# The step size's projection of a hybrid decoder step: from split products on normalized features to plain float32 on the residual stream, in four column groups

## The chip, the cores and the metric

The kernel runs on one core of one Trainium2 chip. The metric is the device time of one execution in microseconds. Before the change it is 954.13 us, the median of three runs (953.25 to 955.27). Beside the times there is one profiled execution, read by views: a page, and questions to its trace (timelines by engine, waits, stretches of time). In these views PE is TensorE's matmul, PEld its weight load, DVE is VectorE, ACT ScalarE, POOL GpSimd, SP SyncE with its DMA queue.

## The reference

One layer of a decoder: a half-step feed-forward stage, a mixer of two parallel parts (a causal pooling mixer and a state-space mixer), and a second half-step feed-forward stage, with 512 prompt tokens and 8 single new tokens, 1024 features, all in float32. The change touches one small product: the last 16 columns of the mixer's input projection, which become the step size of each of the 16 heads.

```python
def _rms_norm(x, g):
    xf = x.astype(jnp.float32)
    y = xf * lax.rsqrt(jnp.mean(xf * xf, axis=-1, keepdims=True) + EPS)
    return (y * g.astype(jnp.float32)).astype(x.dtype)
...
    h = h + 0.5 * _swiglu(_rms_norm(h, ffn1_norm[l]), ...)
    m, p, c, s = _hybrid_mixer(_rms_norm(h, mix_norm[l]), ...)
...
    proj = h @ w_in
    u_pool, z, xbc, dt_raw = jnp.split(
        proj, [POOL_DIM, POOL_DIM + SSD_DIM, POOL_DIM + SSD_DIM + CONV_DIM], axis=-1)
...
    dt = jax.nn.softplus(dt_raw.astype(jnp.float32) + dt_bias.astype(jnp.float32))
```

So the raw step size is `dt_raw = (h * g * r) @ w_dt`, with `g` the norm's 1024 factors and `r` one number for each token.

## The kernel before

Features lie on the 128 partitions, in eight tiles (`k` or `d` from 0 to 7); tokens lie along the free axis, 520 of them in two halves of 260 (`HALVES`). The residual stream is the tile `h`, whose first columns hold the vectors of factors (`vec`).

Most products are made of split operands. A weight unit of 128x1024 is loaded into a staging tile `raw` (four slots in rotation), cast by ScalarE into a high part (`whi`, or `thi` in every third unit) and subtracted by VectorE into a low part (`wlo`, `tlo`; L141). The tiles of the parts come from rotating homes (`weight_homes`). Each product is then three matmuls: high x high, high x low, low x high (`mm3`, L151, L154, L155). The normalized features are split in the same way: `prep` (L179) scales `h` by the norm's factor on ScalarE into `xh` (L182), takes the rest on VectorE into `xl` (L183), squares `h` on ScalarE (L193) and adds the squares on VectorE into `acc` (L194). The factor `r` of each token is applied after the products.

The stage around the change is the seam between the first feed-forward stage and the mixer. The down products `dn` of the first stage run over the eight output tiles; after each one VectorE scales the sum (`td`, L618), adds it to `h` (L623) and `prep` follows. Then the mixer begins: it opens a pool `mx` (`mp`) in the room that the first stage gives back, loads its constants on SyncE's queue (L909 to L922), and computes the step size's raw value:

- `wdt`, 128 x 8 x 16, is loaded into a slot of `raw` (L946). `w48`, in a rotating weight home, holds for each feature tile 48 columns: the high part of the 16 weights, 16 zeros, the low part. It is zeroed by GpSimd (L949), filled by ScalarE (L950) and VectorE (L951).
- For each half and each `k` there are two matmuls: all 48 columns with `xh` (L957), and the first 16 with `xl` (L956, L959). In PSUM, partitions 0 to 15 then hold the high weights' sums and 32 to 47 the low ones'.
- `rstds` makes `r`: a product of `ones` with `acc` (L210, plain float32), a square root on ScalarE (L213), a reciprocal on VectorE (L214).
- `dv`, 48 x 520, is the PSUM sum times `r` (L963). `token_dt` (L970) multiplies it with the selecting matrix `sel`, 48 x 16: two unit matrices over each other, with zeros between. This product adds the two parts and turns tokens onto partitions.

After the projection come the input products `inbc`, `inx` and so on (`inproj`, L929), each of 48 matmuls, by the plans `CONV_PLAN` and `GATE_PLAN`. The order of instructions on each engine is set by a scheduler that works from a model of times when the program is built; on the chip every engine runs its own instructions in that order, and waits for others by semaphores. A tile of a pool whose room was another's waits for the last use of that one.

Of the kernel before, what the change touches and what calls it, by code (L numbers as in the profile page):

```python
# [10 lines left out]
F32 = mybir.dt.float32  # L11
F32R = mybir.dt.float32r
AF = mybir.ActivationFunctionType
ALU = mybir.AluOpType
# [3 lines left out]
P = 128  # L18
# [3 lines left out]
NT = SEQ + NS  # L22
HB = NT // 2
HALVES = (slice(0, HB), slice(HB, NT))
KD = D // P
# [3 lines left out]
NH = 16  # L29
# [29 lines left out]
VEC = {}  # L59
# [9 lines left out]
def tile_trunk_step(ctx: ExitStack, tc: tile.TileContext, ins: dict, outs: dict):  # L69
# [733 lines left out]

    ps[0] = tc.alloc_tile_pool(name="ppm", bufs=8, space=PSUM, reuse_waits="tile")
    mixer(tc, ins, outs, dict(locals()))
    f2["xg"].release()
    xa[0].release()
# [90 lines left out]
def mixer(tc, ins, outs, e):  # L898
    nc = tc.nc
    cst, act, wp, tmp, dr, pool = (e[x] for x in ("cst", "act", "wp", "tmp", "dr", "pool"))  # L900
    ones, queued, squared = e["ones"], e["queued"], tuple(e["added"])
    bank, load_unit, mm3, mm_low_last, ws, v, rstd, rstds, vec, h, nx2, raw_tile, open_f2, fin, fill = (
        e[x] for x in ("bank", "load_unit", "mm3", "mm_low_last", "ws", "v", "rstd", "rstds", "vec", "h", "nx2", "raw_tile",
                       "open_f2", "fin", "fill"))
    xh, xl, _, r = nx2[0]
    xa = e["xa"][0]
    mp = pool("mx", "right")
# [2 lines left out]
    nc.sync.dma_start(out=ident, in_=ins["ident"])  # L910
    tri = mp.tile([P, P], F32, tag="tri", name="tri")
    nc.sync.dma_start(out=tri, in_=ins["tri"])
    sel = mp.tile([48, NH], F32, tag="sel", name="sel")
    nc.sync.dma_start(out=sel, in_=ins["sel"])
    rcnt = mp.tile([P, PAST], F32, tag="rcnt", name="rcnt")
    nc.sync.dma_start(out=rcnt, in_=ins["rcnt"])
    hv = mp.tile([P, 2, NH], F32, tag="hv", name="hv")
# [27 lines left out]

    wdt = raw_tile("dt")[:, : KD * NH].rearrange("p (k h) -> p k h", k=KD)  # L946
    nc.sync.dma_start(out=wdt, in_=ins["w_dt"])
    w48 = e["weight_homes"](1024, "w48", wp, 3, ("whi", "wlo"))[0][:, : KD * 48].rearrange("p (k h) -> p k h", k=KD)
    nc.gpsimd.memset(w48.bitcast(F32), 0.0)  # L949
    nc.scalar.copy(w48[:, :, :NH], wdt)  # L950
    nc.vector.tensor_tensor(out=w48[:, :, 32:48], in0=wdt, in1=w48[:, :, :NH].bitcast(F32), op=ALU.subtract)  # L951
    dtb = [bank(f"dt{b}") for b in range(2)]
    for b, hs in enumerate(HALVES):
        for k in range(KD):
            if k:
                nc.tensor.matmul(dtb[b][:NH, :HB], w48[:, k, :NH], xl[:, k, hs], start=False, stop=False)  # L956
            nc.tensor.matmul(dtb[b][:48, :HB], w48[:, k], xh[:, k, hs], start=k == 0, stop=k == KD - 1)  # L957
            if not k:
                nc.tensor.matmul(dtb[b][:NH, :HB], w48[:, k, :NH], xl[:, k, hs], start=False, stop=False)  # L959
    rstds(nx2[0], "mx")  # L960
    dv = mp.tile([48, NT], F32, tag="h0", bufs=4, name="dv")
    for b, hs in enumerate(HALVES):
        nc.vector.tensor_tensor(out=dv[:, hs], in0=dtb[b][:48, :HB], in1=r[:48, hs], op=ALU.mult)  # L963
    tok = mp.tile([P, 2, NC + 1, NH], F32, tag="tok", name="tok")
    scr_dt = dr.tile([NH, NS], F32, name="scr_dt")
    scr_acs = dr.tile([NC * NH, CH], F32, name="scr_acs")
# [519 lines left out]
```

## Time and profile before

| | |
|---|---|
| median of three runs | 954.13 us |
| lowest, highest | 953.25, 955.27 us |
| span of the profiled execution, first to last instruction | 951.9 us |
| instructions | 19681 |
| mean granted TensorE clock | 0.997 |
| DMA, mean over the span | 145 GB/s |
| the projection's matmuls (L956, L957, L959), starts | 351.96 to 356.06 us |
| the sums of squares (L210), starts | 355.50 to 356.40 us |
| `dv` (L963), starts | 361.17 and 361.79 us |
| selecting product (L974), starts | 368.18 to 369.2 us |

A line of a timeline reads: start in us from the span's start, duration in us, engine, line, operation, tile written <- tiles read, shape, count, and in brackets the idle time ahead of it with what ended it. Rows that follow each other with the same name are merged, with their count. A matmul in plain float32 shows as two records of one instruction. Since matmuls are pipelined and the ends of their records are modelled, the distance between starts is their price, and not the length of a record.

### The profile page before, as it was taken

What the parts mean: (1) busy time and instruction counts of PE and PEld (TensorE: products, weight loads), DVE (VectorE), ACT (ScalarE), POOL (GpSimd) and SP (SyncE); (2) the same over time, 40 slices, a digit from 0 to 9 for tenths busy, and PEclk for the clock granted to TensorE, in tenths of its full rate; (3) what the DMA queues carried; (4) which work ended last, traced back from release to release, by engine and by line L of the source; (5) the groups of instructions that cost most, each with busy time, mean ns of one, the idle gap of its engine ahead of it and who ended that gap; (6) DMA issues with size and microseconds to landing.
All of it is one profiled execution on the core that took longest, in us unless ns stands there. A gap on an engine that the chain in (4) does not pass through costs nothing.

```text
span 951.9 us, 19681 instructions
## 1 busy us (share of the span) xinstructions
PE 942.5 (99%) x7674; PEld 925.9 (97%) x7674; DVE 852.7 (90%) x1462; ACT 635.7 (67%) x1179; POOL 148.3 (16%) x230
## 2 busy tenths in 40 slices
PE   9999999999999999999999999999999999999996
PEld 8999999999999999999999999999999999999996
DVE  6899899998988688789998998999999999999886
ACT  7777756677566455485668735777776676766774
POOL 0011100100100000046251100111112101122120
PEclk9999999999999999999999999999999999999998
DMA  7666554455553343354264453556666655776552
GB/s 205 187 166 150 143 151 135 115 140 156 134 155 95 86 134 122 92 180 138 91 184 133 141 114 115 138 122 160 163 173 176 163 146 144 171 194 185 145 180 91
DMA packets 53995, 138.35 MB, mean 145 GB/s; under 512 B 7750, under 2 KB 15878, under 8 KB 53902
## 3 DMA queue, kind: packets, MB, share of 16 engines
q1 hardware_dynamic: 39918, 104.19, 34.2%
q0 software_dynamic: 13712, 32.78, 18.7%
q8 instruction: 60, 0.98, 0.4%
q14 instruction: 33, 0.27, 0.1%
q10 hardware_dynamic: 272, 0.13, 0.0%
HBM read 129.74 MB, written 7.34 MB: 144 GB/s over the span
## 4 chain that ended last, share of the span: by engine, by line
PE 44%; DVE 2%; issue 1%; POOL 1%; DMA 1%; ACT 1%; DVEq 0%; ACTq 0%; POOLq 0%
PE A L160 8%; PE BE L160 6%; PE wo L160 5%; PE A L165 4%; PE BE L165 3%; PE wo L165 2%; PE P L311 1%; PE dh L155 1%; PE dh L151 1%; PE dh L154 1%; POOL zs L1068 1%; PE inz L151 1%; PE inz L154 1%; PE inz L155 1%; DMA room<-in_state_ssm 1%
## 5 line engine op out<-in xcount | busy, mean ns | idle before, releaser
L504 ACT COPY ac<-A 128x260 f32<-128x260 f32 x85 | 31.6, 372 | 35.4 <-PE A L155 17.3
L433 DVE TENSOR_TENSOR s<-raw 128x1024 f32<-128x1024 f32 x39 | 47.6, 1222 | 4.4 <-DMA raw<-in_w2gu 2.8
L504 ACT COPY ac<-BE 128x260 f32<-128x260 f32 x41 | 15.4, 376 | 33.6 <-PE BE L165 17.7
L151 PE MATMUL inx<-xh_mx,whi_inx 128*128 128x260 f32 x112 | 31.8, 284 | 0.0
L154 PE MATMUL inx<-xl_mx,whi_inx 128*128 128x260 f32 x112 | 31.6, 282 | 0.0
L155 PE MATMUL inx<-xh_mx,wlo_inx 128*128 128x260 f32 x112 | 31.6, 282 | 0.0
L1027 DVE SCALAR_TENSOR_TENSOR A<-U,h,A 128x544 f32<-128x544 f32 x36 | 29.0, 807 | 1.6 <-ACT A L1025 1.2
L311 PE MATMUL P<-x,raw 128*128 128x260 f32 x128 | 28.9, 385 | 0.2 <-DMA raw<-in_w1gu 0.2
L311 PEld LDWEIGHTS P<-x,raw 128*128 128x128 f32 x128 | 24.4, 192 | 4.2 <-DMA raw<-in_w1gu 0.6
L160 PE MATMUL wo<-catg,whi_wo 128*128 128x260 f32 x192 | 27.4, 285 | 0.0
L1193 ACT ACTIVATE so<-br,sxdt 128x128 f32<-128x128 f32 x64 | 22.8, 376 | 5.8 <-DVE room L1195 5.2
L160 PEld LDWEIGHTS wo<-catg,whi_wo 128*128 128x128 f32 x192 | 24.8, 188 | 0.2
L139 ACT CAST thi<-raw 128x1024 fp32r<-128x1024 f32 (+1 forms) x14 | 14.2, 1012 | 15.7 <-PE wo L160 4.8
L1304 DVE TENSOR_TENSOR h<-wo,h 128x260 f32<-128x260 f32 x48 | 19.2, 422 | 5.0 <-PE wo L165 4.7
L252 DVE TENSOR_TENSOR gs<-gq,gs 128x780 fp32r<-128x780 f32 (+1 forms) x28 | 23.3, 831 | 0.0
L151 PE MATMUL inz<-xh_mx,whi_inz 128*128 128x260 f32 x80 | 23.0, 287 | 0.0
L154 PE MATMUL inz<-xl_mx,whi_inz 128*128 128x260 f32 x80 | 22.7, 284 | 0.0
L155 PE MATMUL inz<-xh_mx,wlo_inz 128*128 128x260 f32 x80 | 22.6, 283 | 0.0
L251 ACT CAST gs<-gq 128x780 fp32r<-128x780 f32 (+1 forms) x28 | 20.6, 735 | 1.2 <-DVE gq L555 0.8
L151 PEld LDWEIGHTS inx<-xh_mx,whi_inx 128*128 128x128 f32 x112 | 21.1, 188 | 0.2 <-issue 0.2
L160 PE MATMUL A<-xth_f,qs 128*128 128x260 f32 x84 | 21.2, 283 | 0.0
L160 PE MATMUL A<-xtl_f,qs 128*128 128x260 f32 x84 | 21.2, 284 | 0.0
(3140 smaller groups left out, 4382.9 us busy)
## 6 DMA issues: line engine op xcount, KB each, us to landing
raw<-in_w2gu SPq DMA_DIRECT2D x44, 512.0 KB, 4.4
raw<-in_w1gu SPq DMA_DIRECT2D x41, 512.0 KB, 4.3
raw<-in_w_in SPq DMA_DIRECT2D x24, 512.0 KB, 3.7
raw<-in_w1d SPq DMA_DIRECT2D x16, 512.0 KB, 4.6
raw<-in_w2d SPq DMA_DIRECT2D x16, 512.0 KB, 4.6
raw<-in_w_out SPq DMA_DIRECT2D x12, 512.0 KB, 3.5
ab<-scr_acs SPq DMA_DIRECT2D x8, 512.0 KB, 5.5
h<-in_state_ssm SPq DMA_DIRECT2D x16, 256.0 KB, 3.7
```

Source lines behind the costliest of these rows:

```text
L151: first = nc.tensor.matmul(ps, whi, xhi, start=start, stop=False, **kw)
L154: nc.tensor.matmul(ps, whi, xlo, start=False, stop=False, **kw)
L155: nc.tensor.matmul(ps, wlo, xhi, start=False, stop=stop, **kw)
L160: mm = nc.tensor.matmul(ps, w, x, start=start, stop=False, **kw)
L165: nc.tensor.matmul(ps, w, xhi[k], start=False, stop=k == len(wlo) - 1, **kw)
L251: cast = nc.scalar.copy(hi, s)
L252: low = nc.vector.tensor_tensor(out=lo, in0=s, in1=hi.bitcast(F32), op=ALU.subtract)
L311: mm = nc.tensor.matmul(self.banks[f, u][b][:, :HB], ws(self.raw[f][:, u], j + 4 * q), xg[:, slot[q]], start=j == q == 0, stop=j == 3 and ...
L433: nc.vector.tensor_tensor(out=s1, in0=diag, in1=up0, op=ALU.add)
L504: self.copied = nc.scalar.copy(keep, out[:, :HB]).ins
L1027: nc.vector.scalar_tensor_tensor(out=A[:, :n], in0=U[:, j : j + n], scalar=w(j), in1=A[:, :n], op0=ALU.mult, op1=ALU.add)
L1193: nc.scalar.activation(out=o[:, q], in_=br, func=AF.Copy, scale=sxdt[:, j, b : b + 1]))
```

## The change

The raw step size is no longer made from the split, scaled features `xh` and `xl`, but from `h` itself in plain float32, with the norm's factors multiplied into the weights. The 16 columns are padded with zeros to 32 (`w32`, in the mixer's own pool, zeroed by GpSimd and filled by one multiplication on VectorE). Feature tile `k` writes the group of 32 PSUM partitions that begins at 32 x (`k` mod 4), so that each half has eight matmuls in four groups, each group summing two feature tiles. `dv` then has 128 partitions, and `sel` four copies of a unit matrix over 16 zero rows, loaded in four pieces; the selecting product adds the four groups.

```diff
-    sel = mp.tile([48, NH], F32, tag="sel", name="sel")
-    nc.sync.dma_start(out=sel, in_=ins["sel"])
+    sel = mp.tile([P, NH], F32, tag="sel", name="sel")
+    for g in range(4):
+        nc.sync.dma_start(out=sel[32 * g : 32 * g + 32], in_=ins["sel"][:32])
...
-    w48 = e["weight_homes"](1024, "w48", wp, 3, ("whi", "wlo"))[0][:, : KD * 48].rearrange("p (k h) -> p k h", k=KD)
-    nc.gpsimd.memset(w48.bitcast(F32), 0.0)
-    nc.scalar.copy(w48[:, :, :NH], wdt)
-    nc.vector.tensor_tensor(out=w48[:, :, 32:48], in0=wdt, in1=w48[:, :, :NH].bitcast(F32), op=ALU.subtract)
+    w32 = mp.tile([P, KD, 32], F32, tag="w32", name="w32")
+    nc.gpsimd.memset(w32, 0.0)
+    mix = vec[:, VEC["mix_norm"] : VEC["mix_norm"] + KD]
+    nc.vector.tensor_tensor(out=w32[:, :, :NH], in0=wdt, in1=mix.unsqueeze(2).to_broadcast([P, KD, NH]), op=ALU.mult)
     dtb = [bank(f"dt{b}") for b in range(2)]
     for b, hs in enumerate(HALVES):
         for k in range(KD):
-            if k:
-                nc.tensor.matmul(dtb[b][:NH, :HB], w48[:, k, :NH], xl[:, k, hs], start=False, stop=False)
-            nc.tensor.matmul(dtb[b][:48, :HB], w48[:, k], xh[:, k, hs], start=k == 0, stop=k == KD - 1)
-            if not k:
-                nc.tensor.matmul(dtb[b][:NH, :HB], w48[:, k, :NH], xl[:, k, hs], start=False, stop=False)
+            g = slice(32 * (k % 4), 32 * (k % 4) + 32)
+            nc.tensor.matmul(dtb[b][g, :HB], w32[:, k], h[:, k, hs], start=k < 4, stop=k >= 4, skip_group_check=True)
     rstds(nx2[0], "mx")
-    dv = mp.tile([48, NT], F32, tag="h0", bufs=4, name="dv")
+    dv = mp.tile([P, NT], F32, tag="h0", bufs=4, name="dv")
     for b, hs in enumerate(HALVES):
-        nc.vector.tensor_tensor(out=dv[:, hs], in0=dtb[b][:48, :HB], in1=r[:48, hs], op=ALU.mult)
+        nc.vector.tensor_tensor(out=dv[:, hs], in0=dtb[b][:, :HB], in1=r[:, hs], op=ALU.mult)
```

The scheduler also sets other instructions in another order, since the projection's weights no longer take a turn in the rotation of weight homes. Three places matter for what follows.

TensorE, from the last down product to the first input product, in the changed program (`dt` is the projection's PSUM, `w` its weights, `psr_mx` the sum of squares):

```order
L154 MATMUL dn_7_2_4232<-g_19_3628,whi_1d_2_4228 128x260
L155 MATMUL dn_7_2_4232<-g_19_3628,wlo_1d_2_4229 128x260
L957 MATMUL dt_4317<-h,w_4314 32x260 x8
L957 MATMUL dt_4318<-h,w_4314 32x260 x8
L210 MATMUL psr_mx_4335<-acc_mx,ones 128x260
L210 MATMUL psr_mx_4339<-acc_mx,ones 128x260
L151 MATMUL inbc_4368<-xh_mx,whi_inbc_4364 128x260
L154 MATMUL inbc_4368<-xl_mx,whi_inbc_4364 128x260
```

Sixteen matmuls stand where 32 stood, all ahead of the two sums of squares; before, the last two of them stood between the sums. The first input product's weights are now in `whi_inbc` instead of `thi`.

VectorE, from the last scaled down product (`td_7`) to the reciprocals, what stood there and what stands there now (`wlo_inbc` and `tlo` are low parts of input weights):

```order
 L618 SCALAR_TENSOR_TENSOR td_7_2_4269<-dn_7_2_4232,r_f_90 128x520
 L623 TENSOR_TENSOR h<-td_7_2_4269,h 128x260 x2
-L977 MEMSET dt_v 128x16
+L141 TENSOR_TENSOR wlo_inbc_4536<-raw,whi_inbc_4535 128x1024
+L975 MEMSET dt_v 128x16
 L183 SCALAR_TENSOR_TENSOR xl_mx<-h,xh_mx 128x260
+L952 TENSOR_TENSOR w_4314<-raw,h 128x8x16
 L194 TENSOR_TENSOR acc_mx<-acc_mx,sq_mx_7_4274 128x260
 L183 SCALAR_TENSOR_TENSOR xl_mx<-h,xh_mx 128x260
 L194 TENSOR_TENSOR acc_mx<-acc_mx,sq_mx_7_4280 128x260
```

The low part of the third input weight now stands right behind the last residual add, and the multiplication that makes the projection's weights behind it and the first of the two last `xl`. Before, the subtraction that made them stood far ahead, behind `td_5`. The low part of the second input weight (`tlo`) moves from behind `td_6` to behind the last `acc`.

SyncE's queue, from the step-size weights to the pooling weights, in the changed program:

```order
L948 DMA raw<-in_w_dt 128x128
L147 DMA raw<-in_w_in 128x1024 x4
L910 DMA ident<-in_ident 128x128
L912 DMA tri<-in_tri 128x128
L915 DMA sel<-in_sel 32x16 x4
L917 DMA rcnt<-in_rcnt 128x15
L919 DMA hv<-in_hv 128x32
L921 DMA spool<-in_state_pool 128x480
L923 DMA sconv<-in_state_conv 128x288
L147 DMA raw<-in_w_in 128x1024 x2
L1042 DMA raw<-in_w_pool 128x512
```

Five input weights stood ahead of the constants, and four do now; `sel` is four issues instead of one. The input weight that went behind the constants is the one whose slot of `raw` the step-size weights hold until they are multiplied.

## The prediction

> **What bounds the kernel now.** I read the page's first two parts, then the waits of TensorE, then the timelines of each engine around the step size's projection. The page comes first: busy time by engine and the clock that TensorE was granted.
>
> ```profile
> PE 942.5 (99%) x7674; PEld 925.9 (97%) x7674; DVE 852.7 (90%) x1462; ACT 635.7 (67%) x1179; POOL 148.3 (16%) x230
> PEclk9999999999999999999999999999999999999998
> ```
>
> TensorE is busy 99% of a span of 951.9 us, at full clock in every slice but the last. Its longest waits are these (engine, line, releaser: us in total, times, longest):
>
> ```profile
> PE warm L709 <- DVE eps L95: 1.1, 1, 1.1
> PE factor L870 <- PE psl L864: 0.6, 1, 0.6
> PE inz L151 <- DVE zs L1284: 0.3, 1, 0.3
> ```
>
> The first two stand at the start and at the end of the kernel; between them no wait is longer than 0.3 us. So the time is the sum of what TensorE does, and there is almost no later wait in which a delay could be absorbed: a microsecond added to or taken from TensorE at 350 us should arrive at the end whole. The place itself, on TensorE (start, us, engine, line, operation):
>
> ```profile
> 351.84 0.28 PE L155 MATMUL dn<-g,wlo_1d 128*128 128x260 f32 x1
> 351.96 0.28 PE L957 MATMUL dt<-xh_mx,whi_w 128*48 128x260 f32 x1
> 352.08 0.28 PE L959 MATMUL dt<-xl_mx,whi_w 128*16 128x260 f32 x1
> ...
> 355.38 0.28 PE L957 MATMUL dt<-xh_mx,whi_w 128*48 128x260 f32 x1
> 355.50 0.60 PE L210 MATMUL psr_mx<-acc_mx,ones 128*128 128x260 f32 x2
> ...
> 356.18 0.60 PE L210 MATMUL psr_mx<-acc_mx,ones 128*128 128x260 f32 x2
> 356.42 0.47 PE L151 MATMUL inbc<-xh_mx,thi 128*128 128x260 f32 x1
> 356.73 0.28 PE L154 MATMUL inbc<-xl_mx,thi 128*128 128x260 f32 x1
> ```
>
> Matmuls overlap in their records, so the price of one is the distance between starts: 0.12 us here. From the last down product (351.84) to the projection's first matmul is one such step, so nothing is waited for. The 32 matmuls of the projection take 32 x 0.118 = 3.79 us. A product of `ones` with the squares is plain float32 and shows as two records; the second starts at 356.18, and the second matmul after it at 356.73, so it ends at 356.73 - 0.12 = 356.61: 0.44 us in two passes of 0.22 us. Projection and both sums hold TensorE from 351.96 to 356.61, 4.65 us.
>
> **What is removed and added on TensorE.** Out go 32 matmuls, 3.79 us. In come 16 plain float32 matmuls on 260 columns, two passes each: 32 passes of 0.22 us, which one after the other are 7.0 us. They write four groups of 32 PSUM partitions in turn. What groups are worth is shown by another product of this kernel, `yd`: eight float32 matmuls on 128 columns whose outputs alternate between the lower and the upper 64 partitions. Beside it stands `yo`, of the same length with all 128 columns of weights:
>
> ```profile
> 445.30 1.06 PE L1256 MATMUL yo<-BC,hst 128*128 128x128 f32 x8
> 446.19 1.02 PE L1259 MATMUL pst<-xw,bt 128*128 128x512 f32 x2
> ...
> 430.40 1.09 PE L1262 MATMUL yd<-ab,xdt 128*64 128x128 f32 x16
> 431.43 0.39 PE L151 MATMUL inp<-xh_mx,thi 128*128 128x260 f32 x1
> 431.65 0.28 PE L154 MATMUL inp<-xl_mx,thi 128*128 128x260 f32 x1
> ```
>
> Eight passes of `yo` take 0.89 us, 0.111 us each; sixteen of `yd` take 1.03 us to the next matmul, 0.064 us each, where one after the other they would need 1.78. So two groups do run at once. Four have no row. The bounds are 7.0 us (no overlap) and 32/4 x 0.22 = 1.76 us (all four); I take the lower end, as `yd` reaches the full factor of two except at its borders: 8 rounds of 0.11 are 0.88, and the next matmul counts from 431.65 - 0.12 = 431.53, so the borders cost 0.25 us. The projection then takes 1.76 + 0.25 = 2.0 us, 1.8 less than before. If that were all, the kernel would come to 952.3, just under 0.2% faster.
>
> The Trainium skill, "TensorE: Matmul & The Clock Gate", section "Part 3: Packing small matmuls — row/col tiling", speaks against the lower end: it says that matmuls start and end strictly in program order. `yd` with its two groups takes the same time with and without that rule and cannot decide it. What such an order would make of the time is among the rivals.
>
> **What is late: the weights.** Before, the projection's weights lay in one of the rotating weight tiles, free early; they were zeroed and split eight microseconds ahead. Now they lie in a new tile of the mixer's pool, whose room is the feed-forward stage's until its last product is done. GpSimd's zeroing shows both cases:
>
> ```profile
> 343.47 0.42 POOL L949 MEMSET whi_w<- 128x384 f32 x1 [44.61 <-PE dn L154]
> 351.11 0.10 POOL L1018 MEMSET U<- 128x3 f32 x1 [7.22 <-PE dn L155]
> ```
>
> The zeroing of 256 elements moves behind the second row: 351.2 to about 351.6, or, as the instruction ahead of it now waits for VectorE too, at the latest behind the residual add that ends at 353.66: 354.1. It is then not what is last, for the multiplication that makes the weights is queued on VectorE behind more. VectorE and ScalarE as they stand:
>
> ```profile
> 349.28 1.22 DVE L141 TENSOR_TENSOR tlo<-raw,thi 128x1024 fp32r<-128x1024 f32 x1
> 350.42 0.48 DVE L183 SCALAR_TENSOR_TENSOR xl_mx<-h,xh_mx 128x260 fp32r<-128x260 f32 x1
> 350.82 0.43 DVE L194 TENSOR_TENSOR acc_mx<-acc_mx,sq_mx 128x260 f32<-128x260 f32 x1
> ...
> 352.16 0.70 DVE L618 SCALAR_TENSOR_TENSOR td<-dn,r_f 128x520 f32<-128x520 f32 x1 [0.18 <-PE dn L155]
> 352.89 0.77 DVE L623 TENSOR_TENSOR h<-td,h 128x260 f32<-128x260 f32 x2
> 353.62 0.07 DVE L977 MEMSET dt_v<- 128x16 f32 x1
> 353.91 0.49 DVE L183 SCALAR_TENSOR_TENSOR xl_mx<-h,xh_mx 128x260 fp32r<-128x260 f32 x1 [0.22 <-ACT xh_mx L182]
> ...
> 355.05 0.42 DVE L194 TENSOR_TENSOR acc_mx<-acc_mx,sq_mx 128x260 f32<-128x260 f32 x1
> ```
>
> ```profile
> 352.04 1.05 ACT L139 CAST whi_inbc<-raw 128x1024 fp32r<-128x1024 f32 x1 [1.44 <-PE dn L154]
> 344.25 0.29 DVE L951 TENSOR_TENSOR whi_w<-raw,whi_w 128x128 fp32r<-128x128 f32 x1
> ```
>
> In the new order VectorE does, after the residual add: the low part of an input weight (1.22 us; it needs the cast, done at 353.09), the small memset, one `xl` of 260 columns, and only then the multiplication. An operation's successor starts 0.08 us before its end, as 350.42 after 349.28 + 1.22 shows. So: low part from 353.58 to 354.80; `xl` from 354.78, its successor 0.40 later; multiplication from 355.18, at the 0.29 us of the subtraction of the same shape that it replaces: 355.47. TensorE, which has finished the down product at 351.96, starts the projection at about 355.55. It stands still for 3.6 us, since every instruction behind the first waits with it: the rest of the projection, both sums of squares, the first input products, whose weights have long been there.
>
> The sums of squares do not add to it: the last accumulation, 355.05 to 355.47 before, moves back by the low part (1.14) and the multiplication (0.25 in steps) but not beyond 357.0, and TensorE reaches them at 355.55 + 2.0 = 357.55. They end at 358.43, and the input products start there instead of at 356.61: 1.8 us late. In one sum: + 3.6 (wait) - 1.8 (shorter projection) = + 1.8 us.
>
> **The edits that cost nothing here.** The cast of the weights (L950) leaves ScalarE; `dv` keeps its 260 columns, and the selecting product its 16, so 128 partitions instead of 48 change no length. The low part of the second input weight moves behind the last accumulation, done about 358.2; TensorE wants it when the first input product's 48 matmuls (5.7 us) are done, at 364.1. If that cover were gone, it would cost its 1.2 us. On SyncE's queue `sel` comes in four pieces:
>
> ```profile
> 353.00 0.43 SPq L914 DMA_DIRECT2D sel<-in_sel  x1
> 354.89 0.43 SPq L922 DMA_DIRECT2D sconv<-in_state_conv  x1
> ```
>
> A step from row to row is (354.89 - 353.00) / 4 = 0.47 us, so three more issues push `rcnt`, `hv`, `spool` and `sconv` and the weights behind them by 1.4 us. One input weight, which waited for the room that the step-size weights hold in the staging tile, is issued behind them at about 356.8; it is the fourth input product's, and TensorE comes to it after three of 5.7 us. At the start of the second feed-forward stage the order sets four matmuls earlier, between output products; what they read is there some microseconds ahead, so I give it nothing.
>
> The sum stands against the profiled execution, 951.9 us; the median of the three runs is 954.13, 2.2 more, which lies around the span and which I leave as it is. 954.13 + 1.8 = 955.9. Since the unknown costs lie above more than below, I put the likeliest case at 956.0, its own range 955.2 to 957.0.
>
> **The rivals.**
> *The clock falls in the wait.* That TensorE runs slower when it has not been used is in the rows of the start and the end (the last two are stretches of one microsecond: busy us of the five engine rows, then the granted clock, third from the right):
>
> ```profile
> 1.06 3.78 PE L709 MATMUL warm<-ones 128*128 128x128 f32 x16 [1.06 <-DVE eps L95]
> 944.93 0.42 PE L870 MATMUL factor<-idt,r_tok 65*128 65x65 f32 x4 [0.60 <-PE psl L864]
> 946.00:947.00 1.00, 0.00 (x0) 0.00 (x0) 1.00 (x3) 0.00 (x0) 0.00 (x0) 1.00 0.25 88
> 947.00:948.00 1.00, 0.00 (x0) 0.00 (x0) 0.96 (x3) 0.00 (x0) 0.00 (x0) 0.53 0.74 251
> ```
>
> The first sixteen passes need 3.57 us to the next, 0.22 each, twice what the same shape needs in `yo`; and about 1.7 us after the last matmul the granted clock goes from 1.00 to 0.5. A standstill of 3.6 us is long enough for that, and regaining the clock took about 3.6 us at the start. At half speed the 2.9 us of projection and sums become up to 3.6 + 1.1 = 4.7: + 1.8 on top of + 1.8, 957.7. Against it: TensorE was nearly idle from 942.8 on, so the fall may need over 4 us. The Trainium skill, same page, section "Part 1: The HAM clock gate (the "warmup" mystery)", names an idle window of about 3.4 us with a free-running phase; by that the fall is possible in some executions and not in others, and no run here shows it inside the kernel.
>
> *The groups run two at a time, or not at all.* The two passes of one matmul share a group and stand next to each other in the program. If every pass waits for the start of the one before it, only the second pass of a matmul and the first of the next overlap: 17 rounds of 0.22, 3.7 us instead of 1.76: + 1.9 more, 957.9. Without overlap 7.0 instead of 1.76: + 5.2 more, 961.2. `yd` speaks against the latter.
>
> *Not slower: the weights are not late.* If the multiplication finds its place before the low part (the zeroing done, nothing else needed), its 355.47 becomes 354.3 or earlier; TensorE still needs the last residual add (353.66) for the eighth matmul, and the sums need the last accumulation (355.47). Then the input products start at about 355.5 + 0.9 = 356.4, 0.2 before now: 953.9. The point from which it decides is a multiplication done by 353.7. Against it speaks the fixed order of VectorE's instructions; a later wait that takes up the delay, of which the waits show none, would end in the same place.
>
> *The edits meant to cost nothing do cost.* Later constants or the low part in the wrong place: up to 1.2 us more, 957.2.
>
> **How the numbers follow.** Likeliest case 0.45; clock 0.25; groups two at a time 0.09, none 0.04; weights not late or delay absorbed 0.12; costs elsewhere 0.05. For range and signs: 0.2% (1.9 us) is about what a measurement of this kernel tells from no change; the three runs lie 2.0 us apart. Slower by more than that, above 956.04: half of the likeliest, the rivals above it, 0.22 + 0.24 + 0.13 + 0.05 = 0.64. Within: 0.23 + 0.11 = 0.33 with the rounding. Faster, below 952.2: 0.03, for the full 1.8 us of the shorter projection with no wait at all. The range 954.6 to 958.6 leaves out the overlap that fails entirely and the lower part of the case without a wait.
>
> **What the changed profile would show.** Right: a TensorE wait of 3 to 4 us before the first `dt` matmul, released by VectorE's multiplication at L952, which starts after a 1.2 us low part and one `xl`; 32 `dt` records in about 2 us, four to a round; the input products' first matmul 1.8 us later than now, the rest as far apart as before. A granted clock under 1 around 355 us makes the clock rival right; `dt` records over 3.7 or 7 us the other. I am wrong in the main point if TensorE's wait there is under 2 us.

## The result and the profile after

| | before | after |
|---|---|---|
| median | 954.10 us (4 runs) | 961.66 us (4 runs) |
| lowest, highest | 953.25, 955.27 | 959.27, 962.61 |
| span of the profiled execution | 951.9 | 957.5 |
| ratio to before, 95% interval | | 1.0071 (1.0054 to 1.0088) |

The kernel became 0.7% slower, about 7 us. The prediction was 956.0 us with a range to 958.6, so the direction was right and the size was not. The profiled execution is the shortest of the four; it has a mean granted clock of 0.996, the three others 0.994. Among all the runs below, one execution of the experiment e12 took 1316.35 us at a mean clock of 0.654; it is left out of every figure.

First the page of the changed kernel, busy time of TensorE and its clock, and then TensorE's waits (engine, line, releaser: us in total, times, longest).

```profile
PE 943.1 (98%) x7674; PEld 924.1 (97%) x7674; DVE 851.9 (89%) x1462; ACT 635.1 (66%) x1178; POOL 148.1 (15%) x230
PEclk9999999999999999999999999999999999999999
```

```profile
PE dt L957 <- DVE w L952: 3.3, 1, 3.3
...
PE BE L160 <- DVE xtl_f L252: 0.9, 1, 0.9
PE A L160 <- DVE xtl_f L252: 0.6, 1, 0.6
...
PE BE L160 <- ACT xth_f L251: 0.5, 1, 0.5
```

The first wait is the predicted one. The three that are new besides belong to another place: the start of the second feed-forward stage, 260 us later. Where the 5.6 us of the two spans lie is read from the starts of the same matmuls in both traces:

| the same matmul | before | after | shift |
|---|---|---|---|
| last down product (L155) | 351.84 | 351.44 | -0.40 |
| second input product (L154) | 356.73 | 359.70 | +2.97 |
| `yd` in the mixer | 430.40 | 433.25 | +2.85 |
| second stage's first product with `qs` (L160) | 624.38 | 630.30 | +5.92 |
| span | 951.9 | 957.5 | +5.6 |

So 3.4 us are lost at the seam and 3.1 at the start of the second stage. The rows of the last two places, before and then after, from the timelines of TensorE:

```profile
624.38 0.28 PE L160 MATMUL A<-xth_f,qs 128*128 128x260 f32 x1
```

```profile
433.25 1.09 PE L1260 MATMUL yd<-ab,xdt 128*64 128x128 f32 x16
...
630.30 0.28 PE L160 MATMUL A<-xth_f,qs 128*128 128x260 f32 x1
```

**The seam.** TensorE of the changed kernel, VectorE beside it, and the granted clock in stretches of one microsecond (third number from the right):

```profile
355.07 2.62 PE L957 MATMUL dt<-h,w 128*32 128x260 f32 x32 [3.34 <-DVE w L952]
357.62 2.10 PE L210 MATMUL psr_mx<-acc_mx,ones 128*128 128x260 f32 x4
359.15 0.71 PE L151 MATMUL inbc<-xh_mx,whi_inbc 128*128 128x260 f32 x1
359.70 0.28 PE L154 MATMUL inbc<-xl_mx,whi_inbc 128*128 128x260 f32 x1
```

```profile
353.18 1.22 DVE L141 TENSOR_TENSOR wlo_inbc<-raw,whi_inbc 128x1024 fp32r<-128x1024 f32 x1
354.34 0.47 DVE L183 SCALAR_TENSOR_TENSOR xl_mx<-h,xh_mx 128x260 fp32r<-128x260 f32 x1
...
354.73 0.28 DVE L952 TENSOR_TENSOR w<-raw,h 128x128 f32<-128x128 f32 x1
```

```profile
355.00:356.00 1.00, 0.93 (x20) 0.57 (x24) 1.00 (x4) 0.79 (x1) 0.00 (x0) 1.00 0.12 11
356.00:357.00 1.00, 1.00 (x16) 0.49 (x12) 1.00 (x2) 0.00 (x0) 0.00 (x0) 0.61 0.61 108
357.00:358.00 1.00, 1.00 (x9) 0.38 (x2) 0.23 (x1) 0.00 (x0) 0.00 (x0) 0.50 1.09 319
358.00:359.00 1.00, 1.00 (x3) 0.79 (x3) 0.00 (x0) 0.11 (x1) 0.20 (x1) 0.50 0.63 142
359.00:360.00 1.00, 1.00 (x6) 0.81 (x5) 0.60 (x1) 0.61 (x2) 0.00 (x0) 0.69 0.93 365
```

The multiplication stands behind the low part and one `xl`, as forecast, and TensorE waits for it. Then, from about 356.2 to 359.6, the clock is at half; the fall comes 1.1 us after TensorE has gone on. What this costs is seen beside a second profiled execution of the same kernel (e14 below), whose clock did not fall:

```profile
355.11 1.97 PE L957 MATMUL dt<-h,w 128*32 128x260 f32 x32 [3.34 <-DVE w L952]
357.01 1.14 PE L210 MATMUL psr_mx<-acc_mx,ones 128*128 128x260 f32 x4
...
358.11 0.28 PE L154 MATMUL inbc<-xl_mx,whi_inbc 128*128 128x260 f32 x1
```

```profile
355.00:360.00 5.00, 4.89 (x53) 3.81 (x54) 4.01 (x7) 1.75 (x3) 0.20 (x1) 1.00 0.63 176
```

The projection takes 357.01 - 355.11 = 1.90 us at full clock and 2.55 with the fall; the sums of squares, ending 0.12 us ahead of the second input product, take 0.98 and 1.96. The fall costs 0.65 + 0.98 = 1.6 us.

**The start of the second stage.** ScalarE before and then after: the cast of the first quarter tile `qs` (L246) and that of the third unit's weights (L396), and what stands behind it.

```profile
590.02 0.61 ACT L246 CAST qs<-raw 128x512 fp32r<-128x512 f32 x1
...
608.23 1.05 ACT L396 CAST whi_2a<-raw 128x1024 fp32r<-128x1024 f32 x1 [0.27 <-PE wo L160]
```

```profile
603.17 0.62 ACT L246 CAST qs<-raw 128x512 fp32r<-128x512 f32 x1 [1.83 <-PE wo L160]
...
612.74 1.05 ACT L396 CAST whi_2a<-raw 128x1024 fp32r<-128x1024 f32 x1 [2.38 <-DMA raw<-in_w2gu]
613.69 0.84 ACT L251 CAST xth_f<-xg_f 128x780 fp32r<-128x780 f32 x1
```

SyncE's queue, 585 to 626 us, names what its weight loads wait for, in the kernel before and then in the changed one:

```profile
SPq L389 <- DVE room L436: 8.3, 1, 8.3
...
SPq L389 <- ACT qs L246: 1.6, 1, 1.6
```

```profile
SPq L389 <- ACT qs L246: 12.4, 1, 12.4
...
SPq L389 <- DVE room L436: 11.5, 2, 10.1
```

`qs`, and beside it the sum tile `room`, lie in the room of the third weight home (`thi`, `tlo`). They read a staging slot of `raw`. Before, the last output unit in the third home started on TensorE at 582 us; after, it is a later unit, which started at 595. `qs` comes 13 us later, released by an output product. So the slot comes free late, the load into it is issued late, its landing is what the cast L396 waits for 2.4 us, and in ScalarE's queue the split of the features (`xth`) stands behind that cast. TensorE waits for `xth`, and for `xtl` behind it.

What this costs differs between executions of the same kernel. From `yd` to the first product with `qs`, the kernel before takes 193.98 us; the changed kernel takes 197.05 in this profile and 198.53 in that of e14 (431.67 to 630.20), 3.1 and 4.6 more.

### The profile page after: what moved, and what is told of

It is laid out like the page before. It is cut to its first block, busy times and chain, and to the rows that moved or that the text cites. A ratio compares the mean times of both kernels' runs of the same rounds, so it can differ in the third digit from the quotient of the medians.

```text
span 957.5 us, 19686 instructions
## 1 busy us (share of the span) xinstructions
PE 943.1 (98%) x7674; PEld 924.1 (97%) x7674; DVE 851.9 (89%) x1462; ACT 635.1 (66%) x1178; POOL 148.1 (15%) x230
## 4 chain that ended last, share of the span: by engine, by line
PE 93%; DVE 2%; DMA 2%; ACT 2%; issue 1%; SPq 0%; DVEq 0%; ACTq 0%
PE A L160 7%; PE BE L160 6%; PE wo L160 4%; PE A L151 4%; PE A L155 4%; PE A L154 4%; PE A L165 4%; PE P L311 4%; PE BE L151 3%; PE BE L154 3%; PE BE L155 3%; PE BE L165 3%; PE wo L165 2%; PE inz L151 2%; PE inx L151 2%; PE inz L154 2%
## 5 line engine op out<-in xcount | busy, mean ns | idle before, releaser
L160 PE MATMUL wo<-catg,whi_wo 128*128 128x260 f32 x160 | 22.9, 285 | 0.0
L155 PE MATMUL inz<-xh_mx,wlo_inz 128*128 128x260 f32 x80 | 22.6, 283 | 0.0
L154 PE MATMUL inz<-xl_mx,whi_inz 128*128 128x260 f32 x80 | 22.6, 282 | 0.0
L160 PE MATMUL A<-xth_f,qs 128*128 128x260 f32 x84 | 21.2, 283 | 0.0
L160 PE MATMUL A<-xtl_f,qs 128*128 128x260 f32 x84 | 21.2, 284 | 0.0
L160 PEld LDWEIGHTS wo<-catg,whi_wo 128*128 128x128 f32 x160 | 20.7, 188 | 0.2
L512 DVE TENSOR_TENSOR BE<-BE,ac 128x260 f32<-128x260 f32 (+1 forms) x41 | 18.4, 449 | 2.2 <-PE BE L155 1.6
L154 PE MATMUL dn<-g,whi_1d 128*128 128x260 f32 x72 | 20.0, 281 | 0.0
L151 PE MATMUL dn<-g,whi_1d 128*128 128x260 f32 x72 | 20.0, 282 | 0.0
L155 PE MATMUL dn<-g,wlo_1d 128*128 128x260 f32 x72 | 19.9, 282 | 0.0
```

The costliest lines, as they stand in the source:

```text
L151: first = nc.tensor.matmul(ps, whi, xhi, start=start, stop=False, **kw)
L154: nc.tensor.matmul(ps, whi, xlo, start=False, stop=False, **kw)
L155: nc.tensor.matmul(ps, wlo, xhi, start=False, stop=stop, **kw)
L160: mm = nc.tensor.matmul(ps, w, x, start=start, stop=False, **kw)
```

## The experiments

The short names: "early" or "late" are the projection's weights; the "turn" is which weight falls into which rotating home. The ratio is always to the kernel before on the same chip.

**e1, the old turn with late weights.** One home is taken and not used.

```diff
     w32 = mp.tile([P, KD, 32], F32, tag="w32", name="w32")
+    e["weight_homes"](1024, "w48", wp, 3, ("whi", "wlo"))
```

> The changed kernel, with one weight home taken and not used where the old one took its turn, so that all later weights have the homes they had before; the projection's own weights stay late. Theory A (the stalls at the start of the second feed-forward stage, 3.5 us, come from the shifted turn of the weight homes): they go, the wait of 3.3 us and the fall of the clock at the projection stay: about 958.2 us. Rival B (the stalls are a consequence of everything coming 3 us later and of the changed DMA times): they stay, about 961.7 us.

Measured 955.63 us, ratio 1.0021 (1.0010 to 1.0032): 6 us under the changed kernel. The waits at the second stage are gone. The order of VectorE is the old one too, without the low part ahead of the multiplication, so the wait at the seam is 2.52 instead of 3.34 us:

```profile
354.27 1.96 PE L958 MATMUL dt<-h,w 128*32 128x260 f32 x32 [2.52 <-DVE w L953]
```

It comes out under the 958.2 expected: the wait is 0.8 us shorter, and the turn costs more than the 3.5 us of the expectation (4 to 5 in e4).

**e2, early weights and the old turn.**

```diff
-    w32 = mp.tile([P, KD, 32], F32, tag="w32", name="w32")
+    w32 = e["weight_homes"](1024, "w48", wp, 3, ("whi", "wlo"))[0][:, : KD * 32].rearrange("p (k h) -> p k h", k=KD).bitcast(F32)
```

> The changed kernel with the projection's weights in a weight home, as the old ones were: early, and every later weight in its old home. Theory A: no wait for the weights; TensorE waits only for the last residual add and the last sums (under 1.6 us, no fall of the clock), the input products start about 355.9 instead of 356.6 us, and the second stage starts as before: about 953.4 us. Rival B (later stages stall by other parts of the change: four pieces of sel, the lengths of dv): about 956 to 957 us.

Measured 953.58 us, ratio 0.9993 (0.9983 to 1.0002). The four pieces of `sel` and the lengths of `dv` cost nothing that shows. TensorE's rows:

```profile
351.32 0.28 PE L155 MATMUL dn<-g,wlo_1d 128*128 128x260 f32 x1
...
351.53 2.39 PE L957 MATMUL dt<-h,whi_w 128*32 128x260 f32 x32
...
354.26 1.51 PE L210 MATMUL psr_mx<-acc_mx,ones 128*128 128x260 f32 x4 [0.34 <-DVE acc_mx L194]
...
355.73 0.28 PE L154 MATMUL inbc<-xl_mx,thi 128*128 128x260 f32 x1
```

The projection starts at once, but its last matmuls want the last residual add, and the sums want the last squares. The second input product stands at 355.73 instead of 356.73; 0.52 of that this execution was ahead already at the last down product (351.32 against 351.84). So the 1.9 us of a shorter projection bring 0.5.

**e3, early weights and the changed kernel's turn.**

```diff
-    wdt = raw_tile("dt")[:, : KD * NH].rearrange("p (k h) -> p k h", k=KD)
+    dt_home = raw_tile("dt")
+    wdt = dt_home[:, : KD * NH].rearrange("p (k h) -> p k h", k=KD)
...
-    w32 = mp.tile([P, KD, 32], F32, tag="w32", name="w32")
+    w32 = dt_home[:, 512:768].rearrange("p (k h) -> p k h", k=KD)
```

> The changed kernel with the projection's weights in the unused part of the staging slot that holds the loaded step-size weights: early, but the weight homes turn as in the changed kernel. Theory A: no wait at the projection, but the stalls of 3.5 us at the second feed-forward stage: about 956.9 us. Rival B (those stalls follow from the delay ahead of them): with no delay no stalls, about 953.4 us.

Measured 959.37 us, ratio 1.0055 (1.0043 to 1.0067). No delay at the seam, and the stalls are there all the same: rival B falls. It is 2.5 us over the expectation of A: the stalls are larger than the 3.5 us of the expectation (from `yd` to the first product with `qs` it is 198.85 us here, 4.9 more than before), and in this order the low part stands ahead of the last squares and takes the seam's gain. TensorE's longest wait:

```profile
PE psr_mx L210 <- DVE acc_mx L194: 1.2, 1, 1.2
```

**e4, the kernel before with the new turn alone.**

```diff
     w48 = e["weight_homes"](1024, "w48", wp, 3, ("whi", "wlo"))[0][:, : KD * 48].rearrange("p (k h) -> p k h", k=KD)
+    e["weight_homes"](1024, "w48", wp, 3, ("whi", "wlo"))
+    e["weight_homes"](1024, "w48", wp, 3, ("whi", "wlo"))
```

> The kernel before, with two weight homes taken and not used behind the old projection weights, which puts all later weights into the homes they have in the changed kernel; nothing else is edited. Theory A: the seam as before, the stalls at the second feed-forward stage: about 957.6 us. Rival B: as the kernel before, 954.1 us.

Measured 958.25 us, ratio 1.0049 (1.0037 to 1.0061). Nothing of the projection is edited, and 4 to 5 us are lost. In the profiled execution, 4.4 us longer than the one before, 4.3 of them lie between `yd` and the first product with `qs` (198.31 us against 193.98). The same two rows on ScalarE:

```profile
600.79 0.62 ACT L246 CAST qs<-raw 128x512 fp32r<-128x512 f32 x1 [1.87 <-PE wo L160]
611.47 1.04 ACT L396 CAST whi_2a<-raw 128x1024 fp32r<-128x1024 f32 x1 [3.48 <-DMA raw<-in_w2gu]
```

**e13, a third turn.** As e4 with one unused home instead of two; run later, to see whether it is the third home.

> The kernel before with one weight home taken and not used behind the old projection weights (e4 took two). The third home is then used last by the last of the output units, one later than in e4 and the changed kernel and two later than before. Theory A (the second feed-forward stage's first quarter tile and sum tile lie in the room of the third home, and hold a staging slot until it is free): that room is free at about 611 us instead of 603 (e4) and 590 (before), and the start of the stage costs more than e4's 4.6 us: 961 to 966 us. Rival B (another place of the rotation costs in e4): 954 to 957 us.

Measured 964.58 us, ratio 1.0111 (1.0095 to 1.0127). `qs` comes another 8 us later, the load waits longer, and so does ScalarE:

```profile
609.08 0.62 ACT L246 CAST qs<-raw 128x512 fp32r<-128x512 f32 x1 [0.34 <-PE wo L160]
...
620.47 1.05 ACT L396 CAST whi_2a<-raw 128x1024 fp32r<-128x1024 f32 x1 [5.08 <-DMA raw<-in_w2gu]
```

TensorE waits for the split of the features behind that cast, and its clock falls (stretches of five microseconds):

```profile
PE BE L160 <- ACT xth_f L251: 5.1, 1, 5.1
```

```profile
620.00:625.00 5.00, 1.13 (x3) 0.83 (x4) 2.53 (x3) 4.13 (x7) 0.89 (x1) 0.72 0.97 230
625.00:630.00 5.00, 5.00 (x29) 5.00 (x28) 4.71 (x5) 1.81 (x3) 0.00 (x0) 0.59 0.17 30
```

The three turns order themselves: `qs` at 590.0, 600.8 and 609.1 us go with 954.1, 958.3 and 964.6 us. That settles the place, the third home. How much of the delay comes by `qs` and how much by `room`, which lie there together, no run separates. Not all of e13's loss is the delayed load: from 623.2 to 629.1 us matmuls start 0.22 us apart instead of 0.12, which by estimate is 2.7 us, and all four executions have a mean clock of 0.992 or 0.993.

**e5, the changed kernel with its wait filled.** What the added matmuls write is overwritten.

```diff
     dtb = [bank(f"dt{b}") for b in range(2)]
+    for _ in range(26):
+        nc.tensor.matmul(dtb[1][:, :HB], xh[:, 0, :P], xl[:, 1, :HB], start=True, stop=True)
```

> The changed kernel with 26 matmuls of split features, 0.12 us each, set into the wait ahead of the projection; what they write is written over. They take 3.1 of the 3.3 us that TensorE stands still, and nothing else moves. Theory A (the standstill lets the clock fall, at random by 1.6 us or more): the granted clock stays at 1.00, the executions lie close together, about 959.4 us, 1.6 to 2.5 under the changed kernel. Rival B (what is lost beyond the wait is not the clock): 961.7 us and as wide a spread.

Measured 960.44 us, ratio 1.0065 (1.0050 to 1.0079). Inconclusive: the clock stays at 1.00 at the seam, but in the profiled execution it fell at the second stage instead, and four of six executions have a clock of 0.994 or 0.995:

```profile
355.00:360.00 5.00, 4.77 (x52) 3.49 (x52) 4.01 (x7) 2.11 (x3) 0.20 (x1) 1.00 0.61 159
615.00:620.00 5.00, 3.88 (x9) 2.81 (x10) 4.54 (x7) 4.29 (x7) 1.32 (x2) 0.66 0.81 138
```

**e11 and e12, the same with the old turn,** which leaves one place alone where the clock can fall. e11 is e1 with `range(19)`; e12 is e1 again.

> The e1 kernel (late weights, old turn) with 19 matmuls of split features, 2.3 us, set into its wait of 2.5 us. Theory A (the standstill lets the clock fall in some executions): no granted clock under 0.996, executions within the spread of the kernel before, median about 954.4 us, over 1 us under e1. Rival B (the spread of e1 has another cause): as e1, 955.6 us with executions up to 958.

> The e1 kernel again, on the same chip as e11, for the comparison: median about 955.6 us, some executions with a granted clock of 0.994 or 0.995 and 1.5 to 3 us longer than the rest.

Measured 955.26 us (ratio 1.0010, 1.0001 to 1.0020) and 955.63 us, the median of ten (1.0011, 1.0000 to 1.0022). By the clock, theory A holds: of 22 executions of e1 and e12 half have a clock of 0.994 or 0.995, of 11 of e11 none, and of 92 of the kernel before, in all these comparisons, none. Within e1 and e12 the median is 956.5 us with such a clock and 954.2 without, 2.3 us apart. By the medians, e11 is 0.37 us under e12 where over 1 was expected; these executions, spread over 4 to 5 us each, do not separate the two, and a gain in time by the filled wait is not shown.

**e14, the changed kernel again.**

> The changed kernel again, for the clocks of more executions. Theory A (two places where TensorE stands still, each with its chance of a fall of 1.7 us): granted clocks spread from 0.994 to 0.997 and go with the time, about 958 to 959 us without a fall, 959 to 960.5 with one, 961 to 962.5 with two. Rival B (the clock does not explain the spread): times and clocks unrelated.

Measured 961.28 us, ratio 1.0074 (1.0059 to 1.0089). Clocks run from 0.993 to 0.996, but not with the time: 959.66 us at 0.993, 961.72 at 0.996. The mean to three places is a coarse sign: 0.996 stands both for the first profile of this kernel, with a fall at the seam, and for that of e14, whose clock is at 1.00 in every five microseconds from 5 us to 945. The number of falls alone does not explain the spread of single executions. The start of the second stage differs by 1.5 us between these two profiles; whether that is the rest stays open.

**e6 and e7, one group and two,** on e2; here for two groups, for one the 2 is a 1, with `start` and `stop` to match.

```diff
-            g = slice(32 * (k % 4), 32 * (k % 4) + 32)
+            g = slice(32 * (k % 2), 32 * (k % 2) + 32)
```

> The kernel with early weights and the old turn of homes (e2), all eight feature tiles of a half summed in one group of 32 partitions; sel and dv shrink to 32 rows. Theory A (the groups make the overlap): 32 passes of 0.22 us one after the other, 7.0 us; the input products start 4 us later than in e2, about 957.6 us. Rival B (the projection lies in the shadow of the residual's chain whatever its length): 953.6 us.

> As e6, but with two groups in turn (sel and dv of 64 rows). Theory A: two passes at a time, 3.5 us of projection, the input products start about 0.6 us later than in e2: about 954.2 us. Rival B: as e2, 953.6 us.

Measured 958.82 us (ratio 1.0045, 1.0030 to 1.0059) and 955.28 us (1.0013, 1.0001 to 1.0024), with the projection in 7.1 and 3.7 us. One group, two groups:

```profile
351.60 7.20 PE L957 MATMUL dt<-h,whi_w 128*32 128x260 f32 x32
358.73 1.14 PE L210 MATMUL psr_mx<-acc_mx,ones 128*128 128x260 f32 x4
```

```profile
351.57 3.72 PE L957 MATMUL dt<-h,whi_w 128*32 128x260 f32 x32
355.23 1.14 PE L210 MATMUL psr_mx<-acc_mx,ones 128*128 128x260 f32 x4
```

With the 1.90 us of four groups that is 7.1, 3.7 and 1.9: overlap is complete each time, apart from 0.1 to 0.2 us at the borders.

**e8, the sums behind the first 24 input products,** on e2.

```diff
             for k in range(KD):
                 mm3(bs[b][:, :HB], ws(wh, k), ws(wl, k), xh[:, k, hs], xl[:, k, hs], k == 0, k == KD - 1)
+            if name == "bc0" and b == 0:
+                sums()
...
-    rstds(nx2[0], "mx")
...
+    def sums():
+        rstds(nx2[0], "mx")
...
```

> The e2 kernel with the two sums of squares and what hangs on them behind the first 24 input products instead of ahead of all of them. Theory A (with early weights the shorter projection gains little because TensorE then waits for the last sums): the input products start at once behind the projection, some 1.3 us earlier than in e2: about 952.3 us. Rival B (the norm's factor then comes 2.5 us later and holds up VectorE's reads of the input products): 953.6 us or more.

Measured 954.54 us, ratio 1.0002 (0.9992 to 1.0011). Neither theory as stated: the input products do start at once behind the projection, but nothing is gained; B's time fits, but the waits of TensorE list none between 345 and 375 us that would speak for its mechanism. The scheduler set the projection's last two matmuls singly among the input products.

```profile
354.59 0.28 PE L151 MATMUL inbc<-xh_mx,thi 128*128 128x260 f32 x1
...
354.80 0.63 PE L959 MATMUL dt<-h,whi_w 128*32 128x260 f32 x2
...
355.36 0.39 PE L154 MATMUL inbc<-xl_mx,thi 128*128 128x260 f32 x1
```

From one input product to the next it is 0.77 us instead of 0.12: a lone plain matmul of 32 columns costs 0.65 us here, against 1.90 / 16 = 0.12 in a full set of groups. Of the 0.65 us, 0.44 are its two passes, one after the other, and 0.2 stand at its borders. Twice 0.65 is the 1.3 us that the edit should have given.

**e9 and e10, the first 24 input products first,** then all sixteen matmuls of the projection kept together, then the sums. e9 has early weights (on e2), e10 late ones (on e1).

```diff
             for k in range(KD):
-                mm3(bs[b][:, :HB], ws(wh, k), ws(wl, k), xh[:, k, hs], xl[:, k, hs], k == 0, k == KD - 1)
+                mm3(bs[b][:, :HB], ws(wh, k), ws(wl, k), xh[:, k, hs], xl[:, k, hs], k == 0, k == KD - 1,
+                    pin=name == "bc0" and b == 0)
+            if name == "bc0" and b == 0:
+                dt_and_sums()
...
+    def dt_and_sums():
+        for b, hs in enumerate(HALVES):
+            for k in range(KD):
+                g = slice(32 * (k % 4), 32 * (k % 4) + 32)
+                mm = nc.tensor.matmul(dtb[b][g, :HB], w32[:, k], h[:, k, hs], start=k < 4, stop=k >= 4, skip_group_check=True)
+                tc.keep_in_program_order(mm)
+        rstds(nx2[0], "mx", True)
...
```

> The e2 kernel (early weights, old turn) in another order on TensorE: the first 24 input products, then the sixteen matmuls of the projection without anything between them, then the sums of squares, then the other input products. Theory A (the projection used to cover the last residual add, split and squares; give that cover to the input products and its saving arrives): no wait at the seam, about 1.8 us under the kernel before, 952.3 us. Rival B (the norm's factor 2.3 us later costs at the reads of the input products what is gained): 953.6 us or more.

> The same order with the late weights of the changed kernel (in the mixer's pool; old turn of homes by one unused home). Theory A: the multiplication is done at about 354.2 us, before TensorE comes to the projection at about 354.9; no wait, no fall of the clock, as e9: 952.3 us. Rival B (late weights cost in any place): over 953.5 us.

Measured 952.87 us (ratio 0.9985, 0.9973 to 0.9997) and 952.79 us (0.9983, 0.9973 to 0.9992): 1.4 to 1.5 us under the kernel before, which on that chip took 954.26. It is the only order of those tried in which the saving of the projection arrives. The time of e9 alone does not exclude its rival B (953.6), but the traces do: from the last down product to `yd` e9 takes 76.95 us and e10 76.78, the kernel before 78.56, so 1.6 and 1.8 of the 1.9 us arrive there. TensorE of e10:

```profile
355.64 1.97 PE L964 MATMUL dt<-h,w 128*32 128x260 f32 x32
```

Late weights cost nothing there, and no wait stands ahead of the projection.

## Why the prediction was wrong

- **What bounds the kernel:** right. TensorE is at 98 to 99%, and the delay of the seam stands unchanged at `yd` 75 us later.
- **The late weights:** right. Forecast were a wait of 3.6 us and a multiplication behind a low part and one `xl`; the wait measured 3.3 (3.5 as the forecast counts, from 351.56 to 355.07), with the multiplication just there.
- **The shorter projection:** right, with four groups at once: forecast 2.0 us, measured 1.90. The rivals of two groups at a time and of none are refuted by the same row, and e6 and e7 show what these would have been. The Trainium skill, "TensorE: Matmul & The Clock Gate", section "Part 3: Packing small matmuls — row/col tiling", says that matmuls start and end strictly in program order; here, where the two passes of one matmul share a group, the four groups overlapped fully (1.90 us, where the rival built on that order had 3.7), so that rule did not decide. The overlap of column tiles in that section of the Trainium skill agrees.
- **The seam in sum:** right where the clock holds. The forecast was + 1.8; the execution in the profile of e14 is 0.35 us ahead at the last down product (351.49 against 351.84) and 1.27 behind at `yd` (431.67 against 430.40), so 1.6.
- **The clock, a rival at 0.25:** its mechanism was right and its price too (1.8 forecast, 1.6 measured). Its chance was too low: the clock fell in the first profile, and e1 and e12, with a wait of only 2.5 us, show the lower mean clock in 11 of 22 executions. The argument against it, that the fall at the kernel's end came only after over 4 us, misled, because that end is a single case. The Trainium skill, same page, section "Part 1: The HAM clock gate (the "warmup" mystery)", gives an idle window of about 3.4 us with a phase of its own. A fall in some executions and not in others, and about 3.4 us at half clock, agree with it; the lower mean clocks with a wait of 2.5 us do not fit a window that must be idle throughout.
- **The step that failed:** "the order sets four matmuls earlier, between output products; what they read is there some microseconds ahead, so I give it nothing". I looked at the four matmuls and what they read. What the shifted turn changed was the room of the third home, and with it when `qs` and `room` could be written, when a staging slot came free, and when a load could be issued. e4 shows that this alone costs 4 to 5 us, where the sum had nothing, and e13 that it grows with the delay of that room.
- **The sum mended:** 1.0 to 2.0 us for the seam with its clock at random (e12 and e1, by the ratios), 0.8 for the longer wait of this order (3.3 against 2.5), 4.2 to 4.7 for the turn (e4, by the medians and by the ratio): 6.0 to 7.5. Measured are 6.8 by the ratio and 7.6 by the medians. The forecast had the sign for the right reason, the wait at the seam; the greater part of the size comes from the term that it put at nothing.
- **Had the weights not been late:** the rival said 953.9, e2 measured 953.6. The 1.8 us less of projection could not be had by early weights alone, since the old projection had covered the chain from the last residual add over the split to the last squares.

## What to carry to other kernels

A tile that leaves a rotation, or joins it, shifts every later tile of that rotation. For each room that changes its holder, ask who takes it over next, what that one holds meanwhile (here a staging slot), and which in-order queue stands behind it, as far as the end of the rotation and not only near the edit. A shorter piece of work on the bounding engine gains only what it did not cover: move work that is ready into its place first. And keep small matmuls that share the array in groups together, since one alone among others costs several times its share.

## What the runs showed of the hardware that was not expected

- The clock can fall without one long standstill. In e5 TensorE's waits at the start of the second stage (605 to 626 us) are these, the first two with a single matmul between them, and the clock still went to 0.66 between 615 and 620 us. In e1 and e12 the wait is 2.5 us and half of the executions show the lower mean, in e11, with that wait filled, none; after the wait of 5.1 us in e13 all four do.

```profile
PE A L160 <- ACT xth_f L251: 1.8, 1, 1.8
PE A L160 <- DVE xtl_f L252: 0.6, 1, 0.6
PE BE L160 <- DVE xtl_f L252: 0.3, 1, 0.3
```

- Four groups of 32 columns in plain float32, two passes a matmul, run at 1.90 us for 32 passes of 0.22 us: 3.7 times as fast as one group's 7.1.
